# RWKV triangular inverses: one DRAM tile per key block, small tiles for each direction's first chunk, GpSimd's arithmetic moved to VectorE and ScalarE

## The chip, the cores and the metric

One core of a Trainium2 chip runs the whole program. The metric is device time in microseconds (us) of one execution; the program has one launch and returns a 256x1024 output.

## The reference, cut to what matters

The program is a two-layer hybrid block over 256 latent and 256 context tokens of width 1024. Layer 0 is a gated linear recurrence beside windowed attention, then a dense SwiGLU. Layer 1 runs an S5 state-space mixer beside an RWKV-7 mixer (8 heads of 64, both directions), one output projection, and a top-2-of-8 expert SwiGLU. The change is in the RWKV mixer, whose recurrence per head and direction is

```
def _rwkv7_scan(r, w, k, v, a, b, s0):
    """S_t = S_{t-1} diag(w_t) + (S_{t-1} a_t) b_t^T + v_t k_t^T ; o_t = S_t r_t."""
    def step(s, inp):
        rt, wt, kt, vt, at, bt = inp
        sa = jnp.einsum('bhij,bhj->bhi', s, at)
        s = s * wt[:, :, None, :] + sa[..., None] * bt[:, :, None, :] + vt[..., None] * kt[:, :, None, :]
        return s, jnp.einsum('bhij,bhj->bhi', s, rt)
    ...
def finish(o, r, k, v, g):      # per head: normalise, scale and shift, add the bonus, gate
    m = jnp.mean(o, -1, keepdims=True)
    var = jnp.mean(jnp.square(o - m), -1, keepdims=True)
    o = (o - m) * lax.rsqrt(var + RWKV_GN_EPS)
    o = o.reshape(b, l, R_WIDTH).astype(g.dtype) * lnx_g + lnx_b
    bonus = (jnp.sum(r * k * r_k, -1, keepdims=True) * v).reshape(b, l, R_WIDTH).astype(g.dtype)
    return (o + bonus) * g
```

## The kernel before, in words

**Chunks.** The 512 steps of each direction are cut into 8 chunks of 64. Within a chunk the recurrence needs the inverse of a unit triangular 64x64 matrix for each of the 8 heads; 2 directions x 8 chunks x 8 heads are 128 matrices, one for each SBUF partition.

**Keys.** `rwkv_prep` (L1520) walks over 4 key blocks i (two heads each) and, in `products`, over both directions d. Each (i, d) makes a tile X (decayed keys, written to DRAM `drx`) and a masked Gram matrix G (L1627; one buffer, tag `rG`). L1628 sends G to one DRAM tile `drg` through SP's queue, 8 writes in all.

**Inverse.** `rwkv_inverse` (L1701) loads all of `drg` by one DMA (L1709, 2 MB) into `rM`, sets the diagonals to one (L1710), and inverts all 128 matrices by block doubling with some 100 small VectorE instructions on 128 partitions (L1734 to L1747). The tile `rM` lies in SBUF memory that the key stage used (pool `rC`, closed at L943). Transposed 32x32 blocks go out as `rW`: ScalarE copies them (L1715, L1751), `drw` receives them from GpSimd's queue (L1716) and ScalarE's (L1752), and the inverses go to `dry` through ScalarE's queue (L1749).

**Units.** There are 16 units (chunk step i = 0 to 7, direction d), in the order of `SEQ`. `unit_before` (L1762) loads X of its chunk into `uX` (2 buffers, SP's queue), forms Gram products on TensorE, masks them on VectorE (`lk` L1801; `lk` and `uz` L1793, L1794 for latent chunks), and for i < 7 builds a diagonal decay matrix `udl` on GpSimd (L1806, one buffer) that TensorE multiplies into X (`ztr`); ScalarE evacuates that (`zh`, L1811). For latent chunks GpSimd also multiplies X by r (L1785) and copies the product back (L1786). `unit_inverse` (L1814) loads `uW` and `uY` back from `drw` and `dry` through ScalarE's queue and joins the blocks on TensorE (`pi`). `rwkv_units` (L1838) is the recurrence over i: `pq`, `pz`, `ph` on TensorE, evacuations between them, and a decayed old state `ulT` on GpSimd (L1913), to which VectorE adds `ph` (L1918).

**Around them.** `rwkv_gates` (L1671) has six 128x512 GpSimd operations (L1697 to L1699, twice); `rwkv_finish` (L1934) four (L1945, L1946, twice); `s5` (L1363) four 128x256 additions (L1454) and its loads `wb`, `U`, `E`, `top`, `ca` on GpSimd's queue (L1377 to L1381; `ca` has one buffer).

**Order.** Each engine runs its queue in order. The order within a queue is laid out ahead of time by the framework's planner from the program's order, the dependencies and its own estimates; `MIX` and `ORDER` (L30, L31) set where units, gates (g), first inverses (i) and S5 steps (s) stand in the program: one unit among the last input blocks, then five units, the two first inverses, the gates, and six S5 steps. PSUM banks of the units come from three slots in turn (`mx="ABA"`, A with two buffers, B with one).

Of the kernel before, what the change touches and what calls it, by code (L numbers as in the profile page):

```python
# [8 lines left out]
F32 = mybir.dt.float32  # L9
# [3 lines left out]
AF = mybir.ActivationFunctionType  # L13
# [152 lines left out]
class Build:  # L166
# [1196 lines left out]
    def s5(self, sp, yp):  # L1363
        nc, a, tc = self.nc, self.a, self.tc
        V = nc.vector
        m4 = lambda n, shape: sp.tile(shape, F32, name=n, tag="m4", bufs=2)
        gl = []
# [72 lines left out]
        for q in range(4):  # L1440
            p = self.psum_mm()[:, :256]
            raw = sp.tile([128, 4, 128], F32, name="gw", tag="m4", bufs=2)
            nc.sync.dma_start(raw, a["s5_glu_w"][q])
            wh, wl = (sp.tile([128, 4, 128], F32R, name=f"gw{n_}", tag="U", bufs=2) for n_ in "hl")
            nc.scalar.copy(wh, raw)
            V.tensor_sub(wl, raw, wh.bitcast(F32))
            for k in range(4):
                self.mm(p, wh[:, k], gl[k][0], k == 0, False)
                self.mm(p, wh[:, k], gl[k][1], False, False)
                self.mm(p, wl[:, k], gl[k][0], False, k == 3)  # L1450
            o = sp.tile([128, 256], F32, name="o5", bufs=1)
            nc.scalar.activation(o, p, AF.Tanh, scale=0.5)
            y = sp.tile([128, 256], F32, name="yr", bufs=2)
            nc.gpsimd.tensor_add(y, gl[q][0].bitcast(F32), gl[q][1].bitcast(F32))  # L1454
            V.scalar_tensor_tensor(o, o, 1.0, y, op0=OP.add, op1=OP.mult)
            V.tensor_scalar(o, o, 0.5, None, op0=OP.mult)
            if q == 0:
                self.dump("d_s0", o)
            if q == 3:
                self.dump("d_s3", o)  # L1460
            self.to_y1(yp, q, o)
            yield
# [57 lines left out]
    def rwkv_prep(self, rA, rp, prep):  # L1520
# [53 lines left out]
        self.d_x = [self.dram.tile([8, 128, 4, 256], F32, name=f"drx{d}") for d in range(2)]  # L1574
        self.d_g = self.dram.tile([2, 8, 4, 128, 64], F32, name="drg")
        ch = lambda ap: ap.rearrange("p (c t) -> p c t", t=64)
# [33 lines left out]
        def products(i, kk, parts):  # L1610
            for d, (aa, ex, en) in enumerate(parts):
# [15 lines left out]
                V.tensor_mul(G, pg, tri[:, 0, None, :].to_broadcast([128, 8, 64]))  # L1627
                nc.sync.dma_start(self.d_g[d, :, i].rearrange("c p t -> p c t"), G)  # L1628
                nc.scalar.activation(aa, aa, AF.Identity, scale=ka[:, 0, i:i + 1], bias=ka[:, 1, i:i + 1])
# [41 lines left out]
    def rwkv_gates(self, rV, rB):  # L1671
# [12 lines left out]
        for n, pieces in enumerate(self.TILES):  # L1684
# [11 lines left out]
            V.tensor_mul(hv(c), hv(c), b[:, :, None].to_broadcast([128, 8, 64]))  # L1696
            nc.gpsimd.tensor_add(c, c, ln[1])  # L1697
            nc.gpsimd.tensor_mul(c, c, f)
            nc.gpsimd.tensor_mul(f, f, ln[0])  # L1699

    def rwkv_inverse(self, es):  # L1701
# [6 lines left out]
        Mf = M.rearrange("p s t -> p (s t)")  # L1708
        nc.sync.dma_start(Mf, flat(self.d_g))  # L1709
        V.memset(Mf[:, ::65], 1.0)  # L1710
# [3 lines left out]
        W = rp.tile([128, 32, 32], F32, name="rW", tag="rW", bufs=1)  # L1714
        nc.scalar.copy(W, M[:, 0:32, 32:64].rearrange("p s t -> p t s"))  # L1715
        nc.gpsimd.dma_start(dw[:, 32:64], W)  # L1716
        P = rp.tile([128, 512], F32, name="rP", bufs=1)
        for m in (2, 4, 8, 16):
# [24 lines left out]
            for r in range(1, m):  # L1743
                tv = tmp()
                V.tensor_mul(tv[:, :, :r], bc(view(0, r, r, 1), r, m), bc(Pv[:, :, r:r + 1], r, m))
                ov = view(0, m, r, m)
                V.tensor_add(ov, ov, tv[:, :, :r])  # L1747
        self.d_y = self.dram.tile([2, 8, 4, 128, 64], F32, name="dry")
        nc.scalar.dma_start(flat(self.d_y), Mf)  # L1749
        W = rp.tile([128, 32, 32], F32, name="rW", tag="rW", bufs=1)  # L1750
        nc.scalar.copy(W, M[:, 0:32, 0:32].rearrange("p s t -> p t s"))  # L1751
        nc.scalar.dma_start(dw[:, 0:32], W)  # L1752

# [8 lines left out]
    def unit_before(self, i, d, rp, lk, zh, zp=None):  # L1762
# [18 lines left out]
        if lat:  # L1781
            t0 = (ch - 4) * 64
            r = self.r_r[:, :, t0:t0 + 64]
            R = zp.tile([128, 4, 64], F32, name="uRr", tag="uRr", bufs=6)
            nc.gpsimd.tensor_mul(R, X[:, :, 192:256], r)  # L1785
            nc.gpsimd.tensor_copy(X[:, :, 192:256], R)  # L1786
            z = zp.tile([128, 4, 2, 64], F32, name="uz", tag="uz", bufs=6)
# [14 lines left out]
        if i < 7:  # L1802

            dl = rp.tile([128, 4, 128], F32, name="udl", tag="udl", bufs=1)
            dec = self.r_last[:, d, ch]
            nc.gpsimd.tensor_mul(dl, self.ident[:, None, :].to_broadcast([128, 4, 128]),  # L1806
                                 dec[:, :, None].to_broadcast([128, 4, 128]))
            pt = p128(f"ztr{d}{i}")
# [5 lines left out]
    def unit_inverse(self, rp, i, d):  # L1814
# [4 lines left out]
        W = rp.tile([128, 4, 32], F32, name="uW", tag="uW", bufs=2)  # L1819
        nc.scalar.dma_start(W, self.d_w[d, ch].rearrange("i p t -> p i t"))  # L1820
        nc.scalar.dma_start(Y, self.d_y[d, ch].rearrange("i p t -> p i t"))
        pi = self.psum_mx(f"pi{d}{i}")[:, :256].rearrange("p (n a b) -> p n a b", n=2, a=4)
# [15 lines left out]
    def rwkv_units(self, ra, rp, done, inv, room):  # L1838
# [37 lines left out]
        for i in range(8):  # L1876
# [27 lines left out]
            if not last:  # L1904
                for d in range(2):
# [4 lines left out]
                    if i:  # L1910
                        t = rp.tile([128, 4, 64], F32, name="ulT", tag="ulT", bufs=2)
                        for h in range(2):
                            nc.gpsimd.tensor_mul(t[h2(h)], S[h2(h), h], dec[h2(h), :, None].to_broadcast([64, 4, 64]))  # L1913
                    for p, h in heads:
# [19 lines left out]
    def rwkv_finish(self, rp, yp, n):  # L1934
# [9 lines left out]
        b8 = lambda x: x[:, :, None].to_broadcast([128, 8, 64])  # L1944
        nc.gpsimd.tensor_sub(o, o, b8(mv[:, :, 0]))  # L1945
        nc.gpsimd.tensor_mul(self.r_O[:, n], self.r_O[:, n], self.r_f[:, n])  # L1946
        rs = self.rstd(rp, mv[:, :, 1], 8, 64e-5)
# [388 lines left out]
```

## Time and profile before

| what | value |
|---|---|
| median of 3 runs | 2079.07 us (2071.04 to 2089.49) |
| the profiled execution's own time | 2084.47 us |
| its span | 2082.7 us |
| PE busy | 1937.9 us (93%) |
| VectorE (DVE) busy | 1621.9 us (78%) |
| ScalarE (ACT) busy | 1044.0 us (50%) |
| GpSimd (POOL) busy | 172.4 us (8%) |
| HBM read and written | 442.56 MB, 31.98 MB |
| granted TensorE clock, mean | 0.951 |

The profile is of one execution. An engine's busy share is a mean over stages with different limits, so the sections below go by stage: layer 0 and the keys up to about 957 us, the inverse and the units to about 1205 us, the output projection, routing and experts from there on. PE is TensorE's matmuls, PEld its weight loads, SPq, ACTq and POOLq the DMA queues of SyncE, ScalarE and GpSimd. The granted clock is given as a share of 2.4 GHz, so 0.50 is 1.2 GHz.

### The profile page before, as it was taken

The page shows a single profiled execution, that of the slowest core. Times are in us where ns is not written, and L with a number is a line of the kernel's source. Part 1 is how long each engine was busy: PE and PEld are TensorE (multiplying, and loading weights), DVE is VectorE, ACT ScalarE, POOL GpSimd, SP SyncE. Part 2 cuts the span into 40 slices and gives each one's busy share as a digit, 9 for nine tenths or more (in the row PEclk, how much of TensorE's full clock was granted, in tenths as well). Part 3 has the DMA queues.
Part 4 walks back from the last instruction along what each step waited for, and adds up shares of the span by engine and source line. Part 5 has one row for each costly group of instructions (what it writes and reads, how often), then busy time and mean ns, then how long its engine had stood idle before and what let it go on. Part 6 is the DMA issues. An engine that isn't in the chain of part 4 may idle for free.

```text
span 2082.7 us, 31141 instructions
## 1 busy us (share of the span) xinstructions
PE 1937.9 (93%) x11518; PEld 1524.4 (73%) x11518; DVE 1621.9 (78%) x3038; ACT 1044.0 (50%) x1597; POOL 172.4 (8%) x220
## 2 busy tenths in 40 slices
PE   7999999899999998889488878999999999999996
PEld 4766778687788887667377767888887777777774
DVE  3566656699686868797567779899888888888897
ACT  3344434342323233754122346777776767777773
POOL 1000000001010001001353233000000000000000
PEclk9999999999999999889578879999999999999998
DMA  8334312546565645458767468999989899999891
GB/s 312 112 122 136 108 62 61 173 127 200 190 215 173 215 128 153 123 170 294 209 179 176 136 242 307 353 342 344 356 327 341 330 343 336 341 332 342 331 346 71
DMA packets 148817, 476.68 MB, mean 229 GB/s; under 512 B 54080, under 2 KB 72592, under 8 KB 113584
## 3 DMA queue, kind: packets, MB, share of 16 engines
q1 hardware_dynamic: 120784, 428.40, 59.1%
q0 software_dynamic: 9648, 34.93, 5.2%
q10 hardware_dynamic: 18224, 11.27, 2.0%
q8 instruction: 93, 1.52, 0.3%
q14 instruction: 68, 0.56, 0.1%
HBM read 442.56 MB, written 31.98 MB: 228 GB/s over the span
## 4 chain that ended last, share of the span: by engine, by line
PE 80%; DVE 9%; DMA 5%; issue 2%; ACT 2%; POOL 1%; SPq 0%; DVEq 0%; ACTq 0%; POOLq 0%
PE mm L179 50%; PE mx L179 14%; PE ax L179 7%; PE tp L179 3%; PE tp L183 3%; DVE mwl L201 2%; DMA adaw<-in_ada_w_dram 2%; PE ztr L179 1%; POOL udl L1806 1%; PE gram L179 1%; DMA uX<-drx 1%; DVE wl L201 1%; DMA dt<-in_s_ldt_dram 1%; PE pi L179 0%; DMA ca<-d5ca 0%
## 5 line engine op out<-in xcount | busy, mean ns | idle before, releaser
L201 DVE TENSOR_TENSOR mwl<-mraw,mwh 128x1024 fp32r<-128x1024 f32 x522 | 618.1, 1233 | 56.8 <-ACT mwh L197 53.4
L197 ACT CAST mwh<-mraw 128x1024 fp32r<-128x1024 f32 x528 | 520.4, 1051 | 57.4 <-PE mm L179 33.0
L179 PE MATMUL mm<-hh,wl 128*128 128x512 f32 (+1 forms) x744 | 284.3, 383 | 8.8 <-DVE wl L201 8.6
L179 PE MATMUL mm<-hl,wh 128*128 128x512 f32 (+1 forms) x744 | 285.8, 385 | 4.9 <-DVE hl L457 4.9
L179 PE MATMUL mm<-hh,wh 128*128 128x512 f32 (+1 forms) x744 | 285.6, 387 | 1.7 <-ACT hh L456 1.2
L197 ACT CAST wh<-wraw 128x1024 fp32r<-128x1024 f32 x119 | 124.8, 1050 | 318.6 <-PE mm L179 240.4
L201 DVE TENSOR_TENSOR wl<-wraw,wh 128x1024 fp32r<-128x1024 f32 x119 | 145.2, 1221 | 86.3 <-ACT wh L197 80.1
L179 PE MATMUL mm<-mwh,hgh 128*128 128x512 f32 (+1 forms) x768 | 196.7, 378 | 4.0 <-ACT mwh L197 4.0
L179 PE MATMUL mm<-mwl,hgh 128*128 128x512 f32 (+1 forms) x768 | 197.1, 379 | 2.5 <-DVE mwl L201 2.5
L179 PE MATMUL mm<-mwh,hgl 128*128 128x512 f32 (+1 forms) x768 | 196.0, 378 | 0.0
L179 PEld LDWEIGHTS mm<-hh,wl 128*128 128x128 f32 x744 | 142.5, 191 | 37.7 <-DVE wl L201 10.1
L179 PEld LDWEIGHTS mm<-hl,wh 128*128 128x128 f32 x744 | 142.5, 192 | 32.4 <-DVE hl L457 5.3
L179 PEld LDWEIGHTS mm<-hh,wh 128*128 128x128 f32 x744 | 141.3, 191 | 33.3 <-ACT wh L197 4.4
L179 PEld LDWEIGHTS mm<-mwh,hgh 128*128 128x128 f32 x768 | 137.1, 189 | 34.8 <-ACT mwh L197 5.8
L179 PEld LDWEIGHTS mm<-mwl,hgh 128*128 128x128 f32 x768 | 136.1, 189 | 35.6 <-DVE mwl L201 7.4
L179 PEld LDWEIGHTS mm<-mwh,hgl 128*128 128x128 f32 x768 | 136.5, 188 | 28.6
L179 PE MATMUL mx<-mwh,mal 128*128 128x512 f32 x352 | 103.5, 400 | 0.0
L179 PE MATMUL mx<-mwh,mah 128*128 128x512 f32 x352 | 102.2, 400 | 1.2 <-ACT mwh L197 1.1
L179 PE MATMUL mx<-mwl,mah 128*128 128x512 f32 x352 | 98.9, 397 | 0.0
L179 PEld LDWEIGHTS mx<-mwh,mah 128*128 128x128 f32 x352 | 64.1, 188 | 20.1 <-ACT mwh L197 7.5
L179 PEld LDWEIGHTS mx<-mwl,mah 128*128 128x128 f32 x352 | 65.4, 188 | 13.5
L179 PEld LDWEIGHTS mx<-mwh,mal 128*128 128x128 f32 x352 | 64.5, 188 | 12.8
(601 smaller groups left out, 3097.8 us busy)
## 6 DMA issues: line engine op xcount, KB each, us to landing
mraw<-in_moe_w_dram SPq DMA_DIRECT2D x264, 1024.0 KB, 6.0
adaw<-in_ada_w_dram SPq DMA_DIRECT2D x96, 512.0 KB, 4.9
wraw<-in_ev_w_in_dram SPq DMA_DIRECT2D x26, 512.0 KB, 3.7
wraw<-in_ffn_w_gate_dram SPq DMA_DIRECT2D x22, 512.0 KB, 3.8
wraw<-in_ffn_w_up_dram SPq DMA_DIRECT2D x22, 512.0 KB, 4.5
wraw<-in_ffn_w_down_dram SPq DMA_DIRECT2D x22, 512.0 KB, 3.7
wraw<-in_od_w_in_dram SPq DMA_DIRECT2D x19, 512.0 KB, 4.1
d5ca<-ca POOLq DMA_DIRECT2D x32, 144.0 KB, 3.8
```

What stands on the lines that cost most here:

```text
L179: self.nc.tensor.matmul(out, lhsT, rhs, start=start, stop=stop, skip_group_check=True)
L183: self.nc.tensor.transpose(out, in_, self.ident[:p, :p])
L197: self.nc.scalar.copy(hi, raw)
L201: self.nc.vector.tensor_sub(lo, raw, hi.bitcast(F32))
L1806: nc.gpsimd.tensor_mul(dl, self.ident[:, None, :].to_broadcast([128, 4, 128]), dec[:, :, None].to_broadcast([128, 4, 128]))
```

## The change

Three things are done.

- `drg` becomes four DRAM tiles, one for each key block. `rM` is loaded by eight DMAs on SP's queue, two for each block, each of 16 partitions x 16 KB (every eighth partition).
- For each direction's first chunk (unit i = 0), the inverses and the transposed blocks also go to small DRAM tiles of their own (`dryf`, `drwf`), written from 8 partitions each, ahead of the full `dry` and `drw`. All of these writes are on GpSimd's queue now, and so are the loads of `uW` and `uY` for i = 0; those for i > 0 stay on ScalarE's queue and read the full tiles. The second `rW` copy goes from ScalarE to VectorE.
- GpSimd's arithmetic in the RWKV units, the gates, the finish and the S5 gate goes to VectorE (L1454, L1697 to L1699, L1785, L1913, L1945, L1946) and to ScalarE (L1786 as a copy; L1806 as four 128x128 scaled copies for each unit). The two GpSimd operations of the experts' first norm (L2100, L2101) and its share of the weight split (L203) stay.

```diff
-            nc.gpsimd.tensor_add(y, gl[q][0].bitcast(F32), gl[q][1].bitcast(F32))
+            V.tensor_add(y, gl[q][0].bitcast(F32), gl[q][1].bitcast(F32))
...
-        self.d_g = self.dram.tile([2, 8, 4, 128, 64], F32, name="drg")
+        self.d_g = [self.dram.tile([2, 8, 128, 64], F32, name=f"drg{i}") for i in range(4)]
...
-                nc.sync.dma_start(self.d_g[d, :, i].rearrange("c p t -> p c t"), G)
+                nc.sync.dma_start(self.d_g[i][d].rearrange("c p t -> p c t"), G)
...
-            nc.gpsimd.tensor_add(c, c, ln[1])
-            nc.gpsimd.tensor_mul(c, c, f)
-            nc.gpsimd.tensor_mul(f, f, ln[0])
+            V.tensor_add(c, c, ln[1])
+            V.tensor_mul(c, c, f)
+            V.tensor_mul(f, f, ln[0])
...
-        nc.sync.dma_start(Mf, flat(self.d_g))
+        for i in range(4):
+            for h in range(2):
+                src = self.d_g[i].rearrange("d c (h s) t -> h (d c) (s t)", h=2)[h]
+                nc.sync.dma_start(Mf[2 * i + h::8], src)
+
+        rows = [slice(d * 64 + self.SEQ[d][0] * 8, d * 64 + self.SEQ[d][0] * 8 + 8) for d in range(2)]
+        self.d_wf, self.d_yf = ([self.dram.tile([4, 128, n], F32, name=f"dr{m}f{d}") for d in range(2)] for m, n in (("w", 32), ("y", 64)))
+        wf = [t.rearrange("i (h s) t -> (i h) s t", h=2) for t in self.d_wf]
...
+        for d in range(2):
+            nc.gpsimd.dma_start(wf[d][:, 32:64], W[rows[d]])
         nc.gpsimd.dma_start(dw[:, 32:64], W)
...
+        W = rp.tile([128, 32, 32], F32, name="rW", tag="rW", bufs=1)
+        V.tensor_copy(W, M[:, 0:32, 0:32].rearrange("p s t -> p t s"))
+        for d in range(2):
+            nc.gpsimd.dma_start(self.d_yf[d].rearrange("i (h s) t -> (i h) (s t)", h=2), Mf[rows[d]])
+            nc.gpsimd.dma_start(wf[d][:, 0:32], W[rows[d]])
         self.d_y = self.dram.tile([2, 8, 4, 128, 64], F32, name="dry")
-        nc.scalar.dma_start(flat(self.d_y), Mf)
-        W = rp.tile([128, 32, 32], F32, name="rW", tag="rW", bufs=1)
-        nc.scalar.copy(W, M[:, 0:32, 0:32].rearrange("p s t -> p t s"))
-        nc.scalar.dma_start(dw[:, 0:32], W)
+        nc.gpsimd.dma_start(flat(self.d_y), Mf)
+        nc.gpsimd.dma_start(dw[:, 0:32], W)
...
-            nc.gpsimd.tensor_mul(R, X[:, :, 192:256], r)
-            nc.gpsimd.tensor_copy(X[:, :, 192:256], R)
+            V.tensor_mul(R, X[:, :, 192:256], r)
+            nc.scalar.copy(X[:, :, 192:256], R)
...
-            nc.gpsimd.tensor_mul(dl, self.ident[:, None, :].to_broadcast([128, 4, 128]),
-                                 dec[:, :, None].to_broadcast([128, 4, 128]))
+            for p in range(4):
+                nc.scalar.activation(dl[:, p], self.ident, AF.Copy, scale=dec[:, p:p + 1])
...
-        nc.scalar.dma_start(W, self.d_w[d, ch].rearrange("i p t -> p i t"))
-        nc.scalar.dma_start(Y, self.d_y[d, ch].rearrange("i p t -> p i t"))
+        e, dw, dy = (nc.scalar, self.d_w[d, ch], self.d_y[d, ch]) if i else (nc.gpsimd, self.d_wf[d], self.d_yf[d])
+        e.dma_start(W, dw.rearrange("i p t -> p i t"))
+        e.dma_start(Y, dy.rearrange("i p t -> p i t"))
...
-                            nc.gpsimd.tensor_mul(t[h2(h)], S[h2(h), h], dec[h2(h), :, None].to_broadcast([64, 4, 64]))
+                            V.tensor_mul(t[h2(h)], S[h2(h), h], dec[h2(h), :, None].to_broadcast([64, 4, 64]))
...
-        nc.gpsimd.tensor_sub(o, o, b8(mv[:, :, 0]))
-        nc.gpsimd.tensor_mul(self.r_O[:, n], self.r_O[:, n], self.r_f[:, n])
+        V.tensor_sub(o, o, b8(mv[:, :, 0]))
+        V.tensor_mul(self.r_O[:, n], self.r_O[:, n], self.r_f[:, n])
```

## Rows read from the trace of the kernel before

**Rows 1.** Busy time by stage; columns: stretch, length, engines' busy, clock, DMA share, GB/s

```profile
965.90:1003.40 37.50, 22.31 (x179) 17.05 (x178) 36.24 (x120) 7.64 (x11) 18.55 (x15) 0.77 0.88 273
1003.40:1026.20 22.80, 10.82 (x104) 9.13 (x103) 11.09 (x30) 5.15 (x6) 6.64 (x7) 0.50 0.60 195
1026.20:1060.40 34.20, 21.01 (x355) 16.74 (x356) 20.03 (x50) 7.33 (x26) 13.52 (x18) 0.70 0.80 200
1060.40:1205.00 144.60, 129.12 (x1914) 105.32 (x1915) 104.52 (x300) 45.05 (x120) 51.47 (x77) 0.82 0.61 162
1300.00:2082.70 782.70, 757.73 (x3524) 608.41 (x3523) 687.41 (x712) 542.09 (x624) 0.00 (x0) 0.99 0.86 322
```

**Rows 2.** The chain that ended last, 950 to 1062; columns: start, us, what

```profile
953.25 3.84 DMA drg<-rG
957.16 8.40 DMA rM<-drg
...
993.79 9.07 POOL udl L1806
1002.91 2.09 PE ztr L179 x8
1005.02 9.61 DMA uX<-drx
...
1018.03 2.80 POOL udl L1806
...
1026.27 8.99 DMA ca<-d5ca
...
1048.31 5.32 DVE w L1397
```

**Rows 3.** Timeline of VectorE, 940 to 1005; columns: start, us, instruction, [idle before]

```profile
941.76 0.69 DVE L1631 TENSOR_TENSOR rX<-raa,rcs 128x512 f32<-128x512 f32 x1
...
970.52 1.06 DVE L1747 TENSOR_TENSOR rM<-rM,rt 128x64 f32<-128x64 f32 x1
...
979.50 2.04 DVE L1738 TENSOR_TENSOR rt<-rM 128x480 f32<-128x480 f32 x2
981.46 0.65 DVE L1739 TENSOR_TENSOR rP<-rP,rt 128x480 f32<-128x480 f32 x1
...
1001.99 0.42 DVE L1801 TENSOR_TENSOR lk<-gram,tri 64x256 f32<-64x256 f32 x1
```

**Rows 4.** Busy time in 5 us stretches ahead of the load of rM

```profile
940.00:945.00 5.00, 5.00 (x54) 4.16 (x53) 4.24 (x7) 1.05 (x2) 0.00 (x0) 1.00 0.97 298
...
950.00:955.00 5.00, 5.00 (x32) 3.92 (x30) 4.09 (x7) 4.31 (x8) 0.00 (x0) 1.00 0.60 205
```

**Rows 5.** Instruction groups by shape, GpSimd, whole run; busy us, mean ns, idle before

```profile
L1806 POOL TENSOR_TENSOR udl<-ident,rlast 128x512 f32<-128x512 f32 x14 | 24.8, 1772 | 126.8 <-DMA drg<-rG 93.2 <-PE ztr L179 33.5
```

**Rows 6.** The same view: VectorE from 1046 to 1200, ScalarE over the run

```profile
L1918 DVE TENSOR_TENSOR uT<-ulT,ph 64x256 f32<-64x256 f32 x24 | 10.1, 419 | 13.1 <-PE ph L179 11.6 <-issue 1.0
...
L764 ACT ACTIVATE gsq<-go 128x128 f32<-128x128 f32 x16 | 4.7, 298 | 0.1
```

**Rows 7.** DMA issues, 940 to 1075; count, KB each, median us to landing

```profile
uY<-dry ACTq DMA_DIRECT2D x8, 128.0 KB, 5.7
...
drw<-rW POOLq DMA_DIRECT2D x1, 512.0 KB, 3.8
```

**Rows 8.** Timeline of GpSimd while the gates run

```profile
1048.42 2.48 POOL L1698 TENSOR_TENSOR rfc<-rfc 128x512 f32<-128x512 f32 x2
```

**Rows 9.** Timeline of ScalarE and its queue after the inverse, and TensorE's first pi

```profile
1005.51 1.95 ACT L1751 COPY rW<-rM 128x1024 f32<-128x1024 f32 x1
...
1017.98 0.36 ACTq L1752 DMA_DIRECT2D drw<-rW  x1
...
1026.57 0.52 ACTq L1821 DMA_DIRECT2D uY<-dry  x1
...
1036.82 0.64 PE L179 MATMUL pi<-uY,uW 32*32 32x32 f32 x16
```

## The prediction

> **What bounds the kernel now.** I read four views, in this order. The stage table comes first [rows 1]: from 1300 us to the end TensorE is busy 757.73 of 782.70 us at a clock of 0.99, so the experts only start earlier or later and take their length with them. The stretch that can give is 965.9 to 1060.4: TensorE is busy 22.31, 10.82 and 21.01 us in its three parts and runs at 0.50 to 0.77. In the first VectorE is the bound (36.24 of 37.50 us, the inverse); in the other two no engine is. From 1060.4 to 1205 TensorE is busy 129.12 of 144.60 us and VectorE 104.52.
>
> The chain of waits says what fills the first two parts [rows 2]: the last `drg` write lands at 957.09, the 2 MB load of `rM` takes 8.40, then the inverse, a `udl` of 9.07 on GpSimd, a `ztr`, a `uX` load of 9.61, a `udl` of 2.80, a `ca` load of 8.99, and a VectorE addition (`w`) of 5.32. The timelines say why the GpSimd links are so long [rows 3, 5, 8]. The 14 `udl` sum to 24.8; without the two long ones the mean is (24.8 - 9.07 - 2.80) / 12 = 1.08. The 9.07 one stands over back-to-back inverse instructions on VectorE. The other way round, `w` has 128x256 elements, for which 0.42 is usual (the 64x256 row has as many elements per partition [rows 6]), and took 5.32 while two GpSimd operations of 2.48 in all were ending and a like pair followed [rows 2, 8]. Each of the two engines stands still for the other here.
>
> **The change part by part**, summed against the profiled span of 2082.7 us. That execution took 2084.47, 5.4 above the median of 2079.07 and inside the runs' own spread of 18; I take the difference from the median.
>
> *Load of rM.* Six of the eight loads need nothing of the last key block. The memory of `rM` seems free once the last key product is out: the last `rX` multiply ends at 942.4 [rows 3]. So they can go between 943 and 957, but there the DMA engines are 0.97 busy at first and 0.60 near 952 [rows 4]; 1.5 MB more will delay the last G write a little, I take 0.5. After it only 512 KB remain. Nearest rows: 3.84 for a 256 KB write [rows 2], 3.8 for 512 KB, 5.7 under load [rows 7]; I take 4.3, since the engines have less to do then. Gain 8.40 - 4.3 - 0.5 = 3.6; bounds 0 (no load moves) and 8.40 - 3.84 = 4.6. SP's queue issues seven DMAs more; what stands behind them there, input weights, is loaded some 10 us ahead of use.
>
> A rule is to be weighed here. The chain's row has one 128-partition load of 2 MB at 8.40 us, 250 GB/s [rows 2]. The Trainium skill ("DMA: Bandwidth & Descriptors", Rules for kernel authors) advises against cutting one transfer into two over disjoint partition halves: both halves use the same 16 engines, so they serialize. By it the cut itself gives nothing, and the 3.6 us stand or fall with the idle time of the engines before 957; with none, the sum below loses 3.6. That is a rival below.
>
> *Stalls inside the inverse.* Without GpSimd arithmetic the pair at 979.50 (2.04) falls to two of 0.65, and the 1.06 one at 970.52 to at most 0.65 [rows 3]: 0.74 + 0.41, about 1.2. The end of the inverse moves by 3.6 + 1.2 = 4.8.
>
> *udl to ScalarE.* Four copies of 128x128 at about 0.30 [rows 6] are 1.2 instead of 1.08 undisturbed. The 9.07 link looks like the great gain, and is not: the `ztr` at 1002.91 uses the single-buffer slot of the bank turn, which is free only when `lk` ends at 1002.41 [rows 2, 3], an instruction that the planner placed at the end of VectorE's inverse. So this `ztr` moves by 4.8 + 0.4 (1002.91 goes to 997.7), 5.2. The second long `udl` falls from 2.80 to 1.2: 1.6. The remaining ones cost 0.1 each, hidden: ScalarE is busy 5.15 of 22.80 and 45.05 of 144.60 us there [rows 1].
>
> *The uX load of 9.61.* It was issued when the 2 MB `dry` write was (1005.02). Now the load goes at about 999.8, and ahead of `dry` GpSimd's queue has to wait for the `rW` copy on VectorE and issue four small writes, 3 us or so. I take 8.0, gain 1.6; bounds 0 and 9.61 - 5.7 = 3.9. The copy on VectorE I take as 1.4 (two 128x512 at 0.69 [rows 3]; bounds 0.7 and the 1.95 of ScalarE [rows 9]); it is hidden under this load, and without that cover costs 1.4. Up to the S5 step behind the last `ztr`: 5.2 + 1.6 + 1.6 = 8.4.
>
> *Gates.* `w` falls from 5.32 to 0.42: 4.9. The six 128x512 operations cost VectorE 6 x 0.69 = 4.1, mostly in its idle time while the first inverses run; it is busy 20.03 of 34.20 us [rows 1]. I take 1 on the path; bounds 0 and 4.1.
>
> *First chunk's own tiles.* Before, the `drw` write stood on ScalarE's queue behind an evacuation that waited for TensorE: 1017.98, though the copy began at 1005.51; the `uY` loads came at 1026.57 and the first `pi` at 1036.82 [rows 9]. Now: inverse over at 998.6, copy 1.4, small writes 3.8, loads 5.7 [rows 7], so data at about 1010. Late next is S5's `ca` load (8.99, now from about 1018), during which TensorE stands idle and can do the `pi`. From the first `pi` to the `w` chain are 10 us of `pi`, evacuations and S5 work; I take half, 5, as gone; bounds 0 and 10. GpSimd's S5 loads stand behind the four new loads for as long as the small writes need, 4 us, before `ca` is due.
>
> *Recurrence and finish.* VectorE gains 24 x 0.42 = 10.1 (`ulT`), 12 x 0.42 = 5.0 (r products, S5 gate) and 4 x 0.69 = 2.8: 18 us, from 104.5 to 122.5 of 144.6 at most [rows 1, 6]. The `ulT` has a cover of 13.1 us in which VectorE waits ahead of `uT` [rows 6]. Of the other 8 I put a quarter on the path: +2; bounds -2 (stalls beside GpSimd go here too) and +10 (no cover for `ulT`). An r product on VectorE waits for its `uX` load with evacuations behind it; that is in the bound.
>
> *Sum.* 8.4 + 4.9 - 1 + 5 - 2 = 15.3 us, 2079.07 - 15.3 = 2063.8. The ends: 1.0 (load), 2.3 (uX), 1 (gates), 5 (pi) and 4 (recurrence) more give 28.6 less, 2050.5; 3.6, 1.6, 3.1, 5 and 8 the other way give 6 more, 2085.
>
> **The rivals.**
>
> *The recurrence leads.* If the planner lays `pi` and `pq` ahead of the S5 steps, the first `pi` stands at about 1012 instead of 1036.82, and the rest follows with `w`'s 4.9 gone: about 25 + 4.9 - 2 = 28, 2051. For it: no engine is busy there [rows 1]. Against: TensorE's queue is in order, and S5 work stood ahead of `pi` before.
>
> *VectorE takes it back.* All 18 us on the path and 1 to 3 us of waits at r products: 17.3 - 18 - 2 = -3, 2082. For it: 85% of an in-order queue. Against: the 13.1 us of cover.
>
> *The loads do not move.* All eight in flight after 957.09, on the same engines: 2063.8 + 3.6 = 2067.4. This is the one that the skill's page speaks for; the 0.97 in [rows 4] agrees with it, the 0.60 does not.
>
> *The loads wait for each other* (the other side). They write interleaved partitions of one tile; no row shows whether the framework orders such writes. If each waits for the one before, from 957.09, eight at 3.84 end at 987.8 instead of 962.0: 2063.8 + 25.8 = 2089.6; at 5.7 each at 1002.7, 2104.5. From 2.5 us each on the whole gain is gone, from 5.1 on it is 1% slower. Against: they could begin at 943, and then at 3.84 end at 973, 2075.
>
> **How the numbers follow.** Forecast 0.43 (its own range 2054 to 2074), recurrence leads 0.24, VectorE 0.15, loads do not move 0.10, loads in turn 0.08. The range 2050 to 2085 leaves out parts of the first and the last rival. 1% (20.8 us), about what a measurement of this kernel can tell from none, is 2058.3 and 2099.9. Faster: 0.13 of the forecast and 0.22 of the first rival, 0.35. Slower: half of the last and some of VectorE's, 0.08. Same: 0.57.
>
> **What would show it.** Right: `rM` complete near 962; no VectorE instruction of the inverse above 0.7; `ztr` of the fourth unit near 998 right behind its `lk`; `uY` of the first chunk landed near 1010; `w` at 0.42; first expert some 15 us earlier. Wrong: eight `rM` loads with gaps of a landing each; `lk` and the fourth `ztr` elsewhere; VectorE busy above 85% with `pq` or `ph` waiting for `uT`; TensorE standing before `pi` for anything but its data. What I can't see is how the planner lays the queues anew; one instruction put early or late at the end of the inverse moves all that follows.

## The result, and the profile after

The changed kernel takes 2089.73 us in the median of 20 runs (2081.27 to 2102.37), the kernel before 2074.77 in as many on the same chip (2061.15 to 2089.49): a ratio of 1.0071 [1.0056, 1.0085]. It is 15 us slower, where 15 us of gain were forecast, and 4.7 us above the upper end of the range; by the 1% of the prediction it counts as the same. Executions of one kernel lie up to 15 us to either side of their median, the longer ones at a lower mean clock (of the kernel after, 2081.27 at 0.957 and 2102.37 at 0.940), so the two profiled ones (spans of 2082.7 before and 2082.1 after) say nothing of the difference; the ratios do, and the traces say where.

From the first expert product on, every profiled execution takes 843.8 to 845.5 us, so what differs lies ahead of it. The last write of `drg` is issued between 948.9 and 956.3 us in the profiled executions (953.25 before, 951.61 after); where a few microseconds matter, times are counted from that write below. The same stages as in [rows 1], of the kernel after:

```profile
965.90:1003.40 37.50, 18.96 (x163) 14.75 (x161) 20.58 (x80) 8.55 (x17) 8.67 (x15) 0.75 0.73 239
1003.40:1026.20 22.80, 14.26 (x112) 11.56 (x112) 22.30 (x69) 8.39 (x22) 3.78 (x6) 0.52 0.77 175
1026.20:1060.40 34.20, 17.91 (x306) 15.44 (x306) 15.48 (x43) 6.18 (x22) 9.31 (x15) 0.60 0.95 258
1060.40:1205.00 144.60, 125.24 (x1954) 103.88 (x1955) 113.63 (x352) 56.31 (x160) 11.28 (x22) 0.85 0.63 165
1300.00:2082.10 782.10, 756.97 (x3520) 607.45 (x3518) 685.99 (x711) 540.85 (x622) 0.00 (x0) 0.99 0.85 322
```

VectorE (the fourth number) falls from 36.24 to 20.58 us in the first stage and doubles from 11.09 to 22.30 in the second: the inverse did not get shorter, it was stretched. VectorE's timeline shows how:

```profile
968.29 0.19 DVE L1754 TENSOR_TENSOR rt<-rM,rP 128x32 f32<-128x32 f32 x1
978.55 0.20 DVE L1751 COPY rM<-rP 128x64 f32<-128x64 f32 x1 [10.06 <-ACT rW L1722]
...
988.51 0.38 DVE L1756 TENSOR_TENSOR rM<-rM,rt 128x224 f32<-128x224 f32 x1
993.52 0.43 DVE L1813 TENSOR_TENSOR lk<-gram,tri 64x256 f32<-64x256 f32 x1 [4.63 <-PE gram L179]
993.98 1.20 DVE L1747 TENSOR_TENSOR rt<-rM 128x480 f32<-128x480 f32 x2
```

Two waits, 10.06 and 4.63 us, stand inside the chain, where no gap was above 0.8 us before. The first is for ScalarE's copy of `rW`, which reads `rM` before VectorE may overwrite it. ScalarE's timeline tells why that copy is late (before, it began at 966.08):

```profile
964.07 0.58 ACT L933 COPY uT<-mm 128x512 f32<-128x512 f32 x1
975.09 0.58 ACT L1693 COPY rfc<-mm 128x512 f32<-128x512 f32 x1 [10.44 <-PE mm L179]
976.11 0.58 ACT L1693 COPY rfc<-mm 128x512 f32<-128x512 f32 x1 [0.43 <-PE mm L179]
976.59 1.92 ACT L1722 COPY rW<-rM 128x1024 f32<-128x1024 f32 x1
978.42 1.07 ACT L1664 COPY rvo<-mx 128x512 f32<-128x512 f32 x2
```

The evacuation of a gate product (L1693) now stands ahead of `rW` in ScalarE's queue, and waits 10.44 us, since TensorE has that product (`mm<-rg,rt`, 974.03) behind a whole input block. Behind `rW` stand the value copies `rvo`; behind their writes, in SP's queue, stand the loads of the units:

```profile
955.55 4.97 SPq L1712 DMA_DIRECT2D rM<-drg  x8
...
979.03 1.03 SPq L1665 DMA_DIRECT2D drv<-rvo  x2
980.11 1.14 SPq L935 DMA_DIRECT2D du<-uT  x2
981.30 1.34 SPq L1786 DMA_DIRECT2D uX<-drx  x2
```

So ScalarE, VectorE and SP's queue stand still together. One stretch of 5 us shows it (last three numbers: clock, DMA share, GB/s): VectorE 0.00 us, the DMA engines 0.01 busy; before, the same stretch has VectorE at 4.94 and the DMA engines at 1.03.

```profile
970.00:975.00 5.00, 5.00 (x23) 3.54 (x21) 0.00 (x0) 0.00 (x0) 0.51 (x1) 1.00 0.01 3
```

The `uX` pair, issued at 970.48 before, comes at 981.30, its Gram product is late, and VectorE waits 4.63 for that. TensorE's row of it, and the first `pi`, which stood at 1036.82 [rows 9]:

```profile
992.36 1.12 PE L179 MATMUL gram<-uX 64*64 64x64 f32 x16 [12.14 <-DMA uX<-drx]
...
1043.44 0.64 PE L179 MATMUL pi<-uY,uW 32*32 32x32 f32 x16
```

There is a third delay, ahead of these two: the load itself. VectorE's first instruction that reads `rM`, in the kernel before and in the kernel after:

```profile
965.91 0.17 DVE L1734 COPY rP<-rM 128x64 f32<-128x64 f32 x1 [5.14 <-DMA rM<-drg]
```

```profile
967.76 0.16 DVE L1743 COPY rP<-rM 128x64 f32<-128x64 f32 x1 [2.33 <-DMA drv<-rvo]
```

From the issue of the load (957.16 before, 955.55 the first of eight) to this instruction it is 8.75 us before and 12.21 after; the eight pieces took 3.5 to 7.6 us each to land. All profiled kernels with one load have 8.6 to 9.4 us here, all with two, four or eight 12.2 to 13.2 (e9 below left out: there VectorE comes to this instruction late for another reason).

The inverse (its end is VectorE's second `rW` copy) is over at 1016.98, some 13 us later than before. Counted from the last `drg` write, VectorE's last instruction on `rM` ends after 50.1 us before and 65.0 after: 3.5 us more up to the start of the inverse, 14.7 in the two waits, 3.3 less in the rest of it. The first `pi` comes 8.3 us later by the same count, and the recurrence's last `pq` comes at 1179.4 instead of 1173.8.

### The profile page after: what moved, and what is told of

Same layout as the page of the kernel before. It is cut to its first block, busy times and chain, and to the rows that moved or that the text cites. A ratio compares the mean times of both kernels' runs of the same rounds, so it can differ in the third digit from the quotient of the medians.

```text
span 2082.1 us, 31171 instructions
## 1 busy us (share of the span) xinstructions
PE 1929.2 (93%) x11518; PEld 1518.0 (73%) x11518; DVE 1624.2 (78%) x3085; ACT 1060.1 (51%) x1660; POOL 114.4 (5%) x164
## 3 DMA queue, kind: packets, MB, share of 16 engines
q8 instruction: 93, 1.52, 0.3%
```

## The experiments

The theory first formed from these rows (called D in some expectations) was that the delay of the inverse alone is the loss: cutting the load of `rM` in eight makes the framework lay the queues another way, and one wait in a ScalarE queue stops three engines. Its rivals: VectorE, loaded with GpSimd's arithmetic, loses the time in the recurrence; or the small tiles and their place in memory do; or the late chain of `uX` loads and `lk` products costs by itself (G). Ratios are to the kernel before; other letters in an expectation stand for the theories as that text words them. Five runs (e2, e5, e9, e13, e17) were meant to take the waits out of the inverse. In each a wait came back elsewhere, so they show what such a repair does, and do not decide between D and its rivals.

**One half alone.** e1_arith takes the kernel before and moves the arithmetic only (all lines of the diff that turn `nc.gpsimd` into `V` or `nc.scalar`, and the four `udl` copies); the load, the writes and the tiles stay.

> The kernel before with the six moves of arithmetic alone (udl, the gates, uRr, ulT, the sums of the finish and of S5 off GpSimd); loads, DRAM tiles, queues and writes stay as before. Theory A (the loss of the change lies in the order of loads and writes: the first rW copy held up on ScalarE, uX loads that land late, first-chunk loads that wait for the full writes): these moves keep what the prediction gave them, 2 to 8 us, so a ratio to before of 0.996 to 0.999; in its trace the gram and ztr stalls are shorter and the inverse ends before 1003. Theory B (the moved arithmetic itself costs more on VectorE and ScalarE than it frees): the whole loss is here, a ratio of 1.005 to 1.009. Theory C (eight loads of rM in place of one, by themselves): as theory A, at or below 1.000.

Ratio 1.0008 [0.9981, 1.0036]. The arithmetic as a whole shows no loss, so most of the loss lies in the rest of the change. The inverse stays whole, with `rW` in its old place and the second copy early:

```profile
964.00 2.08 ACT L1715 COPY rW<-rM 128x1024 f32<-128x1024 f32 x1
999.63 1.93 ACT L1751 COPY rW<-rM 128x1024 f32<-128x1024 f32 x1 [1.02 <-DVE rM L1747]
```

The first `pi` comes at 1025.4, 11 us earlier than before, and yet nothing is gained: something gives it back later.

**The first wait taken away.** e2_rw_dve is the kernel after, with the first copy on VectorE, which no longer waits for ScalarE.

```diff
-        nc.scalar.copy(W, M[:, 0:32, 32:64].rearrange("p s t -> p t s"))
+        V.tensor_copy(W, M[:, 0:32, 32:64].rearrange("p s t -> p t s"))
```

> The kernel after with the first rW copy on VectorE instead of ScalarE. In the trace of after VectorE stood idle 10.06 us for that copy, which ran behind two gate evacuations on ScalarE. Theory A: that stall goes and costs about 1 us of VectorE (the second rW copy took 1.01 us there), the inverse ends 8 to 9 us earlier and the time falls by 4 to 9 us: ratio to before 1.003 (1.002 to 1.005) where the change itself has 1.007. Theories B and C: the ratio stays at 1.006 to 1.008.

Ratio 1.0067 [1.0040, 1.0094]: no gain, where theory A expected 1.003. The wait of 10.06 is gone and another of 12.91 is there, for the Gram product whose `uX` pair still goes out at 981.77; the inverse ends at 1019.45.

```profile
969.49 1.08 DVE L1722 COPY rW<-rM 128x1024 f32<-128x1024 f32 x1
...
995.99 0.43 DVE L1813 TENSOR_TENSOR lk<-gram,tri 64x256 f32<-64x256 f32 x1 [12.91 <-PE gram L179]
...
1019.45 1.01 DVE L1758 COPY rW<-rM 128x1024 f32<-128x1024 f32 x1
```

**The load in one piece.** e3_one_load is the kernel after with one `drg` tile and the old single load.

```diff
-        for i in range(4):
-            for h in range(2):
...
+        nc.sync.dma_start(Mf, flat(self.d_g))
```

> The kernel after with one DRAM tile for the matrices and one load of rM of 2 MB, as before; all else as after. Theory A: the first rW copy is again ahead of the gate evacuations on ScalarE and the uX loads no longer stand behind eight others; the 10 us stall goes, the tail (first-chunk loads that wait for the full writes) stays: ratio 0.999 to 1.004. Theory B: 1.006 to 1.008. Theory C: 0.996 to 1.000, and the first pi comes as early as before (1036.8) or earlier.

Ratio 1.0002 [0.9975, 1.0029]: four tiles and eight loads instead of one of each cost 0.7%, the whole loss. ScalarE and VectorE:

```profile
966.90 2.08 ACT L1719 COPY rW<-rM 128x1024 f32<-128x1024 f32 x1 [0.45 <-DVE rM L1714]
...
1002.60 1.04 DVE L1755 COPY rW<-rM 128x1024 f32<-128x1024 f32 x1
```

The `uX` pair goes out at 971.24. The small tiles are in this kernel and not in e1, and the times are alike. From the second `rW` copy to the first `pi` it is 25.8 us in e1 (1025.4 - 999.63) and 27.6 here (1030.2 - 1002.60), so the small tiles don't shorten that way.

**Memory of their own for uW and uY.** In the kernel after, the small writes leave GpSimd's queue from 1016.90 on, but the loads that read them only at 1036.53:

```profile
1016.90 1.20 POOL L1760 DMA_DIRECT2D dryf<-rM  x1 [16.38 <-DVE rM L1756]
...
1036.53 0.76 POOL L1833 DMA_DIRECT2D uW<-drwf  x1 [6.78 <-DMA drw<-rW]
```

They wait for the full `drw` write, which they don't read: `uW` and `uY` are put where `rM` and `rW` lay. e4_own_memory takes both from a pool that is open before.

```diff
-        Y = rp.tile([128, 4, 64], F32, name="uY", tag="uY", bufs=4)
-        W = rp.tile([128, 4, 32], F32, name="uW", tag="uW", bufs=2)
+        Y = self.ra.tile([128, 4, 64], F32, name="uY", tag="uY", bufs=4)
+        W = self.ra.tile([128, 4, 32], F32, name="uW", tag="uW", bufs=2)
```

> The kernel after with uY and uW in the pool that is open before the inverse, so that they do not lie in memory of rM and rW; all else as after. Theory A: the first-chunk loads are issued when their small writes have landed, near 1025 to 1030 rather than 1036.5, and the first pi comes 5 to 8 us earlier; the 10 us stall stays: ratio 1.003 (1.002 to 1.006). If what holds them is not memory but the lanes of the GpSimd queue or the writes' own landing, they move by under 2 us and the ratio stays at 1.006 to 1.008. Theories B and C expect no change either.

Ratio 1.0073 [1.0048, 1.0098]. The loads now leave at 1027.86 to 1032.62. The inverse is over at 1019.63 in this execution; the first `pi` comes 20.0 us behind that instead of 26.5, the last `pq` 162.5 instead of 162.4: what the pool gives at the first `pi` isn't there at the end. TensorE's next wait is for another load (`uT<-drv`, ahead of the `pq` at 1047.50).

**The order put right by a dependency.** e5_rw_tied makes the gate's evacuation wait for `rW`, by one element copied from it.

```diff
+        self.tok = self.ra.tile([128, 1], F32, name="tok")
+        nc.scalar.copy(self.tok, W[:, 0, 0:1])
...
+            nc.scalar.copy(f[:, 0:1], self.tok)
             nc.scalar.copy(f, pg)
```

> The kernel after, eight loads and all, with the gate evacuations tied behind the first rW copy: one element of rW is copied by ScalarE to a small tile, and from there into the gates' tile ahead of each evacuation, which then overwrites it. So ScalarE takes the rW copy, and one of the value copies whose write stands ahead of uX on SyncE's queue, before it waits for the gates' product. Theory D (the loads cost through the order they bring: ScalarE held 10.4 us by the gates' product, behind it the rW copy, the value copies and with them the uX loads): VectorE's 10 us stall goes, uX loads issue some 8 us earlier, the inverse ends 8 to 12 us earlier and the ratio is 0.999 to 1.004. Theory C (the eight loads by themselves): 1.006 to 1.008 as after.

Ratio 1.0049 [1.0022, 1.0075]. `rW` is at 970.01 and its wait 1.51, but a `du` write held SP's queue for 6.19 us, the `uX` pair came at 979.75, and VectorE waited 10.34 for that Gram product; the inverse ends at 1017.41. The wait moved again.

**How many pieces.** e6_two_loads and e7_four_loads have one `drg` tile and cut the load by partitions.

```diff
+        for r in (slice(0, 64), slice(64, 128)):        # e7: four of 32
+            nc.sync.dma_start(Mf[r], flat(self.d_g)[r])
```

> The one-load kernel with its load cut into two halves by partition; the laid-out order keeps the first rW copy ahead of the gate evacuations. Theory D: as with one load, 0.999 to 1.002. Theory C (cost grows with the loads, 0.007 for seven more): 1.001 to 1.002. The two differ little here; the next run with four loads is its pair.

> The one-load kernel with its load cut into four by partition, all from the one DRAM tile; in the laid-out order the gate evacuations now stand ahead of the first rW copy and the first gram behind the last input block, as in after. Theory D: the loss is there as a whole, 1.005 to 1.008, with ScalarE held about 10 us by the gates' product. Theory C: 3/7 of the loss, 1.002 to 1.004.

Two: 1.0043 [1.0017, 1.0070], `rW` at 968.22 ahead of the gates, the inverse over at 1004.34. Four: 1.0086 [1.0056, 1.0116], gates ahead of `rW` again, waits of 9.74 and 4.41, the inverse over at 1013.67. These read the one old tile, so it doesn't take the four tiles. The run with two is above what either theory expected, and has no wait over 1.52 us in its inverse. But its inverse starts 13.14 us behind its first load (8.89 in e3), and ends, counted from the last `drg` write, 4.0 us later than e3's. That is the pieces' own late landing. The two runs lie 8.5 us apart, with intervals of some 5.5 us to either side of each, so how much of the 8.5 it is can't be said. The two-load kernel's rows:

```profile
954.91 1.14 SPq L1710 DMA_DIRECT2D rM<-drg  x2
```

```profile
968.05 0.16 DVE L1741 COPY rP<-rM 128x64 f32<-128x64 f32 x1 [2.96 <-DMA drv<-rvo]
```

With four it is 12.88 us, and the order that D blames comes on top. A cost in proportion to the number of loads (C) isn't there: two, four and eight have 1.0043, 1.0086 and 1.0071.

**The kernel before, once more.** e8_before_again is unchanged, for the spread of the recurrence.

> The kernel before, unchanged, for a second profile: how far the same stretches differ from one execution to the next. Every theory: the inverse ends within 2 us of 1003.4, the first pi within 3 us of 1036.8; the stretch from the last rG product to the first MoE gather product (286.4 us in the first profile) differs by up to 10 us with the granted clock.

The time was 2070.36. Up to the first `pi` (1038.4 against 1036.82) it is the old trace. From the first to the last `uR` evacuation it takes 113 us at a mean clock of 0.89 in that stretch, where the first profile takes 126 at 0.84. So a recurrence's length in one profile is compared with one at a like clock only.

**All of SP's unit loads out of the way.** e9_uX_rw is e2 with the first six `uX` loads on GpSimd's queue.

```diff
-        nc.sync.dma_start(X[:, :, :n], self.d_x[d][ch][:, :, :n])
+        (nc.gpsimd if i < 3 else nc.sync).dma_start(X[:, :, :n], self.d_x[d][ch][:, :, :n])
```

> The kernel after, eight loads and gate evacuations ahead as they are, with the first rW copy on VectorE and the first six uX loads on GpSimd's queue instead of SyncE's, so that they no longer stand behind the writes of the input blocks (in after the pair that the inverse's third and fourth lk products need was issued at 981.3, in before at 970.5). Theory D (what costs are the two waits for work that stands behind the gates' product on ScalarE: rW, and uX by way of SyncE's queue): with both gone VectorE has no stall over 2 us in the inverse, which ends near 1004 to 1007 instead of 1016.6, and the ratio is 0.998 to 1.003. If the ratio stays at 1.006 to 1.008 with the inverse at 1005, the loss lies behind the inverse instead.

Ratio 1.0072 [1.0032, 1.0112]. Two `lk` products were laid ahead of the `rW` copy on VectorE: waits of 9.42 and 6.33 us, the inverse over at 1024.47.

**Which part of the arithmetic gives, which takes.** e10_udl is the kernel before with `udl` on ScalarE alone, e11_ulT the kernel before with `ulT` on VectorE alone, e12_no_ulT is e1 with `ulT` left on GpSimd.

```diff
 # e10: the four scaled copies instead of the one nc.gpsimd.tensor_mul(dl, ...)
 # e11 alone has, and e12 alone (of e1's lines) has not:
-                            nc.gpsimd.tensor_mul(t[h2(h)], S[h2(h), h], ...)
+                            V.tensor_mul(t[h2(h)], S[h2(h), h], ...)
```

> The kernel before with udl alone on ScalarE (four scaled copies for each). Theory E (what the moves win ahead of the recurrence is lost inside it, because ulT and the products moved to VectorE lengthen it: 122.7 us from the first uR copy to the last with all the moves against 113.1 in the second profile of before, at granted clocks of 0.89 and 0.94): udl is not in the recurrence's chain, the first pi comes 5 to 10 us earlier and that stays: 0.995 to 0.998. Theory F (the end of the recurrence is set by the S5 work that it shares the engines with, whenever the recurrence starts): 0.999 to 1.001.

> The kernel before with ulT alone on VectorE (28 products of 64 rows inside the recurrence). Theory E: this is what takes the gain back, 6 to 10 us: 1.003 to 1.005, and the stretch from the first uR copy to the last is longer than before's at the same granted clock. Theory F: 0.999 to 1.001. The prediction gave the whole recurrence +2 us: 1.001.

> The kernel before with all the moves of arithmetic but ulT's, which stays on GpSimd. Theory E: the gain ahead of the recurrence is kept: 0.995 to 0.998. Theory F: 0.999 to 1.001, as with all the moves (1.0008).

`udl` 0.9964 [0.9928, 1.0001], `ulT` 1.0031 [0.9992, 1.0071], all but `ulT` 0.9961 [0.9924, 0.9998]. Each interval alone reaches 1 or nearly so; the pair e1 (1.0008) against e12 says the same as e11, and e14 below once more. The recurrence is longer in e11's profile too (134 us from first to last `uR` against 126 before), but at a clock of 0.81 against 0.84, so the ratios are the evidence. The group of `uT` on VectorE, 1046 to 1200, of e11, of e12 and of e1, then that of the kernel after with its `ulT`:

```profile
L1918 DVE TENSOR_TENSOR uT<-ulT,ph 64x256 f32<-64x256 f32 x24 | 10.1, 419 | 10.5 <-PE ph L179 10.0
```

```profile
L1918 DVE TENSOR_TENSOR uT<-ulT,ph 64x256 f32<-64x256 f32 x24 | 10.1, 419 | 9.5 <-issue 4.3 <-PE ph L179 3.5 <-POOL ulT L1913 1.2
```

```profile
L1918 DVE TENSOR_TENSOR uT<-ulT,ph 64x256 f32<-64x256 f32 x24 | 10.1, 419 | 2.2 <-PE ph L179 1.7
```

```profile
L1926 DVE TENSOR_TENSOR ulT<-uT,rlast 64x256 f32<-64x256 f32 x24 | 10.1, 420 | 0.7
L1931 DVE TENSOR_TENSOR uT<-ulT,ph 64x256 f32<-64x256 f32 x24 | 10.1, 419 | 2.6 <-PE ph L179 2.1
```

The wait ahead of `uT` is 13.1 us in the first profile of the kernel before [rows 6] and 9.2 in the second, so e11's 10.5 says little. With the rest of the arithmetic moved, it falls with `ulT` on VectorE from 9.5 (e12) to 2.2 (e1), and from 8.0 (e14 below) to 4.0 (e3): much of the wait was used, and the kernel is some 10 us slower all the same. Which instructions are held up by `ulT` isn't shown.

**Eight loads on two queues.** e13_two_queues sends every second load of the kernel after through ScalarE's queue; e15_queues_no_ulT is that with `ulT` on GpSimd, e16_queues_no_ulT_own that with e4's memory as well.

```diff
-                nc.sync.dma_start(Mf[2 * i + h::8], src)
+                (nc.sync if h else nc.scalar).dma_start(Mf[2 * i + h::8], src)
```

> The kernel after with its eight loads of rM dealt over two queues, four on SyncE's and four on ScalarE's; all else as after. In the laid-out order the first rW copy stands ahead of the gate evacuations again and the uX loads ahead of the second input block's write. Theory D (the order costs, not the loads): VectorE's stalls of 10 and 5 us in the inverse are gone, the inverse ends near 1003 and the ratio is 0.998 to 1.002, as with one load (1.0002). Theory C (eight loads cost by themselves): 1.006 to 1.008.

> The kernel after with the eight loads dealt over two queues and ulT back on GpSimd. Theory D and E together: 0.994 to 0.998, faster than before. Theory C: 1.002 to 1.005.

> As the run before, with uY and uW in memory of their own as well. If the first chunk's loads, once free of the full writes, bring the recurrence forward: 2 to 4 us better than the run before. If the first pi is not what the recurrence's end waits for, as own memory alone suggested (1.0073 against 1.0071): the same within 1 us.

e13: 1.0065 [1.0042, 1.0089]. Now `rW` is ahead of the gates (968.74) and three `uX` loads are out by 974.59, but the fourth goes out only at 988.89, and VectorE waits for its product. D's condition, no stall in the inverse, isn't met, and the ratio lies where C expected it:

```profile
1004.27 0.43 DVE L1813 TENSOR_TENSOR lk<-gram,tri 64x256 f32<-64x256 f32 x1 [9.02 <-PE gram L179]
...
1016.13 1.04 DVE L1758 COPY rW<-rM 128x1024 f32<-128x1024 f32 x1
```

e15: 1.0014 [0.9998, 1.0029], between what D with E (0.998 at most) and C (1.002 at least) expected; against e13 `ulT` is worth 0.5% here too. e16: 1.0027 [1.0011, 1.0043], so memory of their own brings nothing, though the first `pi` comes 6 us earlier, counted from the last `drg` write.

**The best of both.** e14_one_load_no_ulT is e3 with `ulT` on GpSimd.

> The kernel after with one load of rM and ulT back on GpSimd. If the two losses are apart and add up: the 1.0002 of one load less the 0.003 to 0.005 of ulT, 0.995 to 0.998. If the loss by ulT was paid only where the loads were as before: 1.000.

2065.76 us, 0.9954 [0.9938, 0.9970]: faster than the kernel before, by 9.0 us of the median, and than the kernel after by 24. The second `rW` copy comes at 999.17, the first `pi` at 1027.3, the last `pq` at 1156.9. Against e3 `ulT` is worth 0.48%, some 10 us.

**The lk products kept out of the inverse.** e17_lk_behind is e2, and e18_one_load_lk_behind is e14, with the `lk` products of the five units after the first made to wait for the end of the inverse, by a mask `tri2` that is `tri` plus zero times `rM`.

```diff
+        V.scalar_tensor_tensor(self.tri2[:, 0], Mf[:, 0:64], 0.0, self.tri[:, 0], op0=OP.mult, op1=OP.add)
...
-        tri = self.tri
+        tri = self.tri2 if (i, d) > (0, 0) and i < 3 else self.tri
```

> The kernel after, eight loads on SyncE's queue as they are, with the first rW copy on VectorE and the lk products of the five units after the first tied behind the inverse (their mask is a copy to which zero times the inverted matrix is added). Theory D (the loss is VectorE's inverse held in queue order): no stall over 3 us in the inverse, which ends near 1001 to 1004 instead of 1016.6, and the ratio is 0.999 to 1.003. Theory G (the late uX loads cost by themselves, since the lk products are late either way): the inverse ends as early but the ratio stays at 1.005 to 1.008. Theory C (eight loads by themselves): as G, 1.006 to 1.008.

> The kernel with one load of rM and ulT on GpSimd (0.9954) with the lk products of the five units after the first tied behind the inverse. Where no lk product holds the inverse, the tie only takes their 4 us out of it: the inverse ends 3 to 4 us earlier; Theory D and E: 0.994 to 0.996. If the units' lk products are what the recurrence's start waits for: 0.997 to 1.000.

1.0116 [1.0079, 1.0153] and 1.0038 [1.0016, 1.0060]. No `lk` stops the inverse any more, but the layout moved an S5 product there instead. VectorE of e17:

```profile
1000.42 0.42 DVE L1118 TENSOR_TENSOR rt<-E,tp 128x256 f32<-128x256 f32 x1 [7.42 <-PE tp L179]
...
1013.01 1.06 DVE L1760 COPY rW<-rM 128x1024 f32<-128x1024 f32 x1
1036.94 0.86 DVE L1815 TENSOR_TENSOR lk<-gram,tri 64x256 f32<-64x256 f32 x2 [14.26 <-PE gram L179]
```

In e18 the same wait is 7.14 and the inverse ends at 1007.64, 8.5 us after e14's. But the kernel is 16.5 us slower than e14: `uX` has two buffers, each free only when its unit is through, so the last load goes out at 1037.1 instead of 1012.5, and the first `pi` comes at 1048.7 instead of 1027.3. In e17 the inverse ends earlier than in the kernel after, and the kernel is slower. So the inverse's end alone does not set the loss: D falls in that form. That the late `uX` loads and `lk` products cost by themselves (G) fits, but isn't shown: the tie makes them later than they are in the kernel after, and in neither run does the inverse end as early as G's test asked.

## Why the prediction was wrong, point by point

- **Load of rM, -3.6: the step that failed, in three ways.** First, when the loads can start. "The memory of `rM` seems free once the last key product is out" was read from VectorE's last `rX`, which ends at 942.4. But the last Gram matrix G is made later, from 952.35 to 953.03, and the write that takes it out of `rG` lands at 957.09. The eight loads were issued in a row from 955.55 on, when that write had landed (951.61 + 3.9); none went early, though six don't read what it wrote. SP's queue names this write as what its loads waited for (1.0 us), and ScalarE's `udl` does too. The last G of the kernel before, and ScalarE in the kernel after:

```profile
952.35 0.68 DVE L1627 TENSOR_TENSOR rG<-mx,tri 128x512 f32<-128x512 f32 x1
```

```profile
955.66 0.99 ACT L1819 ACTIVATE udl<-ident,rlast 128x128 f32<-128x128 f32 x3 [1.64 <-DMA drg<-rG]
```

  The likely reason is that `rG` lies in the pool whose memory `rM` takes over; a place of its own for `rM` was not tried, so that is argued and not shown. Second, what the pieces cost: they landed some 3.5 us later than one load, not earlier. The Trainium skill ("DMA: Bandwidth & Descriptors", Rules for kernel authors) says that halves of a transfer over disjoint partitions share the same engines and serialize. The trace agrees that the cut gains nothing (inverse begun at 967.76 after, 965.91 before), and the runs with two to eight pieces show a cost that the rule does not name: 12.2 to 13.2 us from issue to the start of the inverse, against 8.6 to 9.4. Third, the order: cutting the load made the planner lay several queues another way, with waits of 10.06 and 4.63 us in the inverse. The prediction said that it could not see the new layout, and still priced it at nothing. The rival "the loads do not move" was right that none goes early, and its price of 3.6 left out the second and the third. By e3 against the kernel after, the load costs 0.0069 x 2075 = 14 us.
- **Stalls inside the inverse, -1.2: right where it looked, wrong in sum.** The pair of 2.04 is 1.20 now, and with one load (e1) the inverse takes 35.4 us instead of 37.5, a gain of 2.1. In the kernel after, 10.06 and 4.63 came beside it. "The loads wait for each other" (2089.6) came nearest in time, by luck and not by its mechanism: SP issued all eight within 4.97 us.
- **udl, -5.2 and -1.6, and uX, -1.6: right in direction.** Alone, `udl` gives 0.36%, 7.5 us, against 8.4; its interval reaches from 15 us to nothing. Four copies take 1.28 us (estimated 1.2). In the kernel after, nothing of it can be told apart beside the late loads.
- **Gates, -4.9 + 1: right in the trace, not seen in the time.** The group of `w` had one of 5.40 us among six before; after:

```profile
L1397 DVE TENSOR_TENSOR w<-rt,rt x5: 410/415/419, 1021.0 to 1091.5; 128x256 f32<-128x256 f32 x5
```

  But all moves but `ulT` (e12, 0.9961) give no more than `udl` alone (e10, 0.9964). With intervals of 0.4% a gain of 3.9 us can't be excluded; none is shown.
- **First chunk's tiles, -5: nothing.** The loads wait for the full writes because of where `uW` and `uY` lie. With memory of their own (e4, e16) the first `pi` or its data came earlier and the end did not. The full `dry` write took 14.5 us on GpSimd's queue:

```profile
dry<-rM POOLq DMA_DIRECT2D x1, 2048.0 KB, 14.5
```

- **Recurrence, +2: a term of the right sign, sized too small.** It is +10: 0.48% in e14 against e3, 0.51% in e15 against e13, 0.47% in e12 against e1. Its upper bound was 10, for no cover at all. The wait ahead of `uT` that was to be the cover did shrink (9.5 to 2.2 from e12 to e1), and the 10 us were lost all the same; why stays open. The rival "VectorE takes it back" was true as a part.
- **Sum.** With the terms as measured: load +14, `ulT` +10, the rest of the arithmetic about -8 (e12), the tiles 0: +16, and 15 was measured. This is no independent check, since the load's 14 is itself the kernel after less e3.

What stays open: whether eight loads could cost less in some layout. No layout with four or more ended the inverse before 1013, all with one or two by 1008, and every attempt to put one queue right moved the wait elsewhere. The pieces' own late landing, some 3.5 us, came in every layout with more than one; why they land later isn't shown. Beyond that, the number of loads and the order that comes with it were never parted. Nor is it parted how much of the rest of the 14 us is the inverse and how much the late `uX` chain.

## What to carry to other kernels

Where a planner lays out in-order queues, cutting one DMA into several is an edit of the whole schedule around it, and the pieces can land later than the whole. Look first in the trace at what stands behind each instruction that would be late, and expect a wait taken from one queue to turn up in the next. An idle wait on an engine is no sure cover for work that is moved there: its length differed between two executions of one kernel, and here the wait was used and the kernel still got slower. A buffer that looks free by the engine that used it last may lie in memory that a pool, or a DMA of another tile, still holds; look for what the load itself waits for.

## What the runs showed of the hardware

A 2 MB load of 128 partitions in one DMA let its reader start 8.6 to 9.4 us after its issue; cut by partitions into two, four or eight DMAs, on one queue or on two, 12.2 to 13.2 us after the first issue (other transfers, much the same ones, ran beside it in all cases). The same stretch of the same kernel, the recurrence, took 126 us at a granted clock of 0.84 and 113 at 0.89, so one profile of a stage with TensorE half waiting is a weak witness. Work of one size differs by engine and neighbour: `w` (128x256) took 0.41 us on VectorE with GpSimd silent, and up to 5.40 with GpSimd working; four scaled 128x128 copies on ScalarE took 1.28 us, where GpSimd took 1.03 to 1.45 for all four in twelve of fourteen cases, 2.80 in one, and 9.07 in one over back-to-back VectorE instructions.
